# Hybrid attention and GLA encoder layer: softmax left unscaled, all linear q and k through the seven-product units, out projection split 6 and 10

## The chip, the cores and the metric

One core of one Trainium2 chip runs the whole layer. The metric is the device time of one execution in microseconds; the kernel before has a median of 2158.83 us over three runs.

## The reference

One encoder layer over 512 tokens of width 2048, in float32. A projection of 6176 columns feeds 16 softmax heads of 64 (group A) and four heads of gated linear attention, GLA (group B). Their outputs are concatenated, projected by `w_out`, added to the input, and followed by a SwiGLU of width 5632 and a last RMSNorm.

```
h = rmsnorm(x, attn_norm_w)
aq, ak, av, gq, gk, gv, gr, glr = split(h @ w_in)
# group A: three (window, dilation) patterns per head, merged by their softmax denominators
attn = sum_i softmax_i(lse)[i] * softmax(q k_i^T / 8 + bias) v_i
# group B: chunked gated linear attention, forward and backward, q and k of 4 heads x 128
o = gla(gq * 128**-0.5, gk, gv, gate_fwd) + flip(gla(flip(...), gate_bwd))
gla_out = rmsnorm_per_head(o) * gla_norm_w * silu(gr)
x = x + concat(attn, gla_out) @ w_out
x = x + (silu(h2 @ w_gate) * (h2 @ w_up)) @ w_down        # h2 = rmsnorm(x, ffn_norm_w)
return rmsnorm(x, final_norm_w)
```

Because all three patterns of a head are merged by their denominators, a head is one softmax over 512 keys with a bias that counts the patterns. The kernel computes it so.

## The kernel before

The schedule is written out by hand: the order in the program is the order on each engine. Every operand of a large product is split into a rounded high part (ScalarE, `act.copy`) and a low part (VectorE, a subtraction), and each product is three matmuls: high by high, high by low, low by high.

**Jobs.** A job (`run_job`) is a direct product over 16 blocks of 128 rows with four PSUM banks; one block of weights is a *half* of 12 matmuls with 512 columns. The stream `st` loads weights ahead on SP's queue and splits them. In the order of time: two jobs for the softmax heads' v; the Front stage (below); job "A", which computes the second 256 columns of the linear q and of the linear k directly and whose results `evac_gqk` scales and stores to `gqd`; two jobs for the linear v (`evac_gv`); the first half (rows 0 to 7 of `mixh`, the softmax heads' results) of the out projection for the column blocks 1, 2 and 3; the out projection of block 0 over all 16 rows; the second half of blocks 1, 2 and 3; then SwiGLU and the down projection.

**Front units.** `Front` computes 256 columns of `w_in` for all tokens as a *unit*: four pieces, in each of which two 2x2 block products are done with seven products instead of eight (`products`, lines 1548 and 1562: a matmul of 512 columns and one of 256 each). `evac7` combines the seven sums with ScalarE copies, VectorE additions and four accumulating DMAs of POOL's queue; `finish` multiplies by the row norms and stores to DRAM. Before there are 14 units: the gate r (4), the first half of linear q and k (2), the softmax q and k (8).

**Side work.** While a job runs, `run_side` advances a queue of generators by `rate` steps per half (`RATES`: 3.1 in job A and the gv jobs, 4.0 in the out jobs), after each of its four banks; every call first advances the generator at the head of `urgent` by one step. The side queue holds the low-rank gate (14 steps), then `attention`, then GLA (started in turns).

**Attention.** A step pair of `attention` is one *unit* `u` of 64 (16 heads x 4 query blocks). In unit u: scores on PE (`att_scores`, lines 630 and 631), bias and minimum on VectorE (`att_max`, L640), exponential with its row sum on ScalarE (`att_exp`, L648). Then the row is scaled by the reciprocal of its sum (`att_norm`: reciprocal, L651, and for even units the multiplication, L653, on VectorE; `att_scale` for odd units on ScalarE, L657). Then four transposes (`att_transpose`, L662), the rounded part (`att_round`, L670), the rest (`att_rest`, L676), the product with v for two units at a time (`att_av`, L686 and L687), a copy across partitions (`att_lift`, L696) and the sum into a head pair's result `mixf[pr]` (`att_mix`, L705), which is then split into `mixh[pr]`. `read_qk` loads the next pair's q and k by eight DMAs on POOL's queue (L569), `load_qk` splits them (L592, L588). GLA's last transposes stand at L1132, the split of its results at L922.

**Slots.** SBUF is cut into 36 slots of 512 columns (tiles `a`) and 33 of 1024 (tiles `b`), PSUM into 8 banks (`ps`); each is handed out in the order in which it came free, and its next writer waits for its last reader.

## Time and profile before

| | |
|---|---|
| median of three runs | 2158.83 us (2158.61 to 2159.88) |
| the profiled execution | 2159.02 us, span 2157.2 us |
| granted TensorE clock | 0.999 |
| HBM read and written | 287.47 MB and 66.39 MB |

The profile gives each engine's busy time (PE is TensorE's matmuls, PEld its weight loads, DVE VectorE, ACT ScalarE, POOL GpSimd, SP the queue that loads weights). Matmuls are pipelined and the profile models their ends, so the distance from one start to the next tells what a matmul costs, and the busy time does not. A wait row names the instruction that waited and the one that released it. A landing is the time from a DMA's issue to its completion.

### The profile page before, as it was taken

How to read it: one execution, taken by the hardware profiler on the slowest of the kernel's cores; microseconds unless marked ns; L12 is line 12 of the kernel's file. 1: busy time of each engine (PE TensorE's matmuls, PEld its weight loads, DVE VectorE, ACT ScalarE, POOL GpSimd, SP SyncE). 2: the span in 40 equal slices, each digit the busy share in tenths (PEclk: the TensorE clock that was granted, in tenths of full speed). 3: DMA queues.
4: the chain of work that ended last, by engine and by line, in shares of the span. 5: the costliest groups of instructions: out<-in, count | busy, mean ns of one | idle time of the engine just before them, and what ended most of it. 6: DMA issues, size and time to landing. Idle time of an engine off the chain costs nothing.

```text
span 2157.2 us, 35082 instructions
## 1 busy us (share of the span) xinstructions
PE 2145.5 (99%) x12714; PEld 1896.6 (88%) x12714; DVE 1843.6 (85%) x3187; ACT 1234.4 (57%) x2250; POOL 364.0 (17%) x501
## 2 busy tenths in 40 slices
PE   9999999999999999999999999999999999999998
PEld 7888888888888889888888888888888899999987
DVE  6699999688878788899999998999989888888885
ACT  8455555578876456455555555555555655555562
POOL 0011222211121110022112211221122220021300
PEclk9999999999999999999999999999999999999999
DMA  6367778846575863567677667776677885576982
GB/s 203 136 181 182 179 179 192 245 143 190 174 220 172 279 243 103 149 181 182 181 179 196 173 183 182 178 194 174 180 188 181 260 212 178 179 183 156 282 309 78
DMA packets 266203, 407.55 MB, mean 189 GB/s; under 512 B 19309, under 2 KB 163613, under 8 KB 266030
## 3 DMA queue, kind: packets, MB, share of 16 engines
q1 hardware_dynamic: 206238, 274.59, 39.8%
q0 software_dynamic: 59472, 130.19, 27.1%
q8 instruction: 100, 1.64, 0.3%
q14 instruction: 73, 0.60, 0.1%
q10 hardware_dynamic: 320, 0.53, 0.1%
HBM read 287.47 MB, written 66.39 MB: 164 GB/s over the span
## 4 chain that ended last, share of the span: by engine, by line
PE 56%; DMA 1%; issue 1%; DVE 1%; POOL 0%; ACT 0%; DVEq 0%; ACTq 0%; POOLq 0%
PE ps L1562 25%; PE ps L1548 12%; PE ps L1926 5%; PE ps L1927 5%; PE ps L1925 5%; PE ps L346 1%; PE ps L348 1%; PE ps L347 1%; PE ps L2122 1%; PE ps L2121 1%; PE ps L2120 1%; DMA gd<-b 1%; DMA b<-a 0%; POOL xd L1806 0%; DVE b L1471 0%
## 5 line engine op out<-in xcount | busy, mean ns | idle before, releaser
L1466 ACT CAST b<-b 128x1024 fp32r<-128x1024 f32 (+1 forms) x585 | 533.8, 944 | 386.4 <-DVE b L1471 193.1
L1471 DVE TENSOR_TENSOR b<-b,b 128x1024 fp32r<-128x1024 f32 (+1 forms) x585 | 614.0, 1084 | 34.4 <-ACT b L1466 22.9
L1562 PE MATMUL ps<-b,b 128*128 128x512 f32 x1708 | 500.7, 393 | 0.4 <-ACT b L1466 0.2
L1562 PE MATMUL ps<-a,b 128*128 128x512 f32 x1428 | 418.7, 393 | 0.3 <-DVE b L1582 0.2
L1562 PEld LDWEIGHTS ps<-b,b 128*128 128x128 f32 x1708 | 289.4, 188 | 32.6 <-ACT b L1466 0.6
L1548 PEld LDWEIGHTS ps<-b,b 128*128 128x128 f32 x1708 | 280.6, 190 | 40.8
L1548 PE MATMUL ps<-b,b 128*128 128x256 f32 x1708 | 307.4, 280 | 0.0
L1548 PEld LDWEIGHTS ps<-a,b 128*128 128x128 f32 x1428 | 236.9, 189 | 38.0 <-DVE b L1471 0.5
L1562 PEld LDWEIGHTS ps<-a,b 128*128 128x128 f32 x1428 | 238.5, 188 | 24.1 <-issue 0.6
L1548 PE MATMUL ps<-a,b 128*128 128x256 f32 x1428 | 256.6, 280 | 0.1
L1453 DVE TENSOR_TENSOR b<-b 128x512 f32<-128x512 f32 x268 | 183.6, 685 | 19.0 <-PE ps L1927 7.3
L1926 PE MATMUL ps<-b,b 128*128 128x256 f32 x624 | 176.6, 283 | 0.0
L1927 PE MATMUL ps<-b,b 128*128 128x256 f32 x624 | 176.6, 283 | 0.0
L1925 PE MATMUL ps<-b,b 128*128 128x256 f32 x624 | 176.6, 283 | 0.0
L346 PE MATMUL ps<-b,b 128*128 128x512 f32 x332 | 133.8, 403 | 0.1
L348 PE MATMUL ps<-b,b 128*128 128x512 f32 x332 | 129.8, 391 | 0.1
L347 PE MATMUL ps<-b,b 128*128 128x512 f32 x332 | 129.5, 390 | 0.0
L1454 DVE TENSOR_TENSOR b<-b,b 128x256 f32<-128x256 f32 x268 | 114.0, 425 | 9.3
L1455 DVE TENSOR_TENSOR b<-b,b 128x256 f32<-128x256 f32 x268 | 114.0, 425 | 9.2
L1927 PEld LDWEIGHTS ps<-b,b 128*128 128x128 f32 x624 | 119.8, 192 | 0.0
L1925 PEld LDWEIGHTS ps<-b,b 128*128 128x128 f32 x624 | 119.8, 192 | 0.0
L1926 PEld LDWEIGHTS ps<-b,b 128*128 128x128 f32 x624 | 119.8, 192 | 0.0
(308 smaller groups left out, 4039.8 us busy)
## 6 DMA issues: line engine op xcount, KB each, us to landing
b<-in_w_gate_dram SPq DMA_DIRECT2D x109, 512.0 KB, 3.7
b<-in_w_up_dram SPq DMA_DIRECT2D x88, 512.0 KB, 3.8
b<-in_w_down_dram SPq DMA_DIRECT2D x88, 512.0 KB, 5.4
b<-in_w_in_dram SPq DMA_DIRECT2D x86, 512.0 KB, 3.8
b<-a POOLq DMA_DIRECT2D x168, 256.0 KB, 4.5
b<-in_w_out_dram SPq DMA_DIRECT2D x32, 512.0 KB, 6.3
gd<-b POOLq DMA_DIRECT2D x22, 512.0 KB, 4.0
b<-gd SPq DMA_DIRECT2D x22, 512.0 KB, 8.3
```

What stands on the lines that cost most here:

```text
L346: mm(o, xh.t[:, c], wh.t[:, w], start=first and not on, stop=False, skip_group_check=on)
L347: mm(o, xh.t[:, c], wl.t[:, w], start=False, stop=False, skip_group_check=on)
L348: mm(o, xl.t[:, c], wh.t[:, w], start=False, stop=last, skip_group_check=on)
L1453: dve.tensor_tensor(s_[:, :, 0:2], r[:, :, 1:3], r[:, :, 0:1].to_broadcast(shape), op=OP.add)
L1454: dve.tensor_tensor(s_[:, :, 2], s_[:, :, 0], r[:, :, 2], op=OP.add)
L1466: act.copy(o, src)
L1471: dve.tensor_tensor(o, src, h, op=OP.subtract)
L1548: mm(o, wl, xh, start=False, stop=end, skip_group_check=True)
L1562: mm(o.rearrange("p (s t) -> p s t", s=2), wh, x_, start=first and p == 0, stop=False, skip_group_check=True)
L1925: mm(o, xh[:, t], wh, start=first and h == 0, stop=False, skip_group_check=True)
L1926: mm(o, xh[:, t], wl, start=False, stop=False, skip_group_check=True)
L1927: mm(o, xl[:, t], wh, start=False, stop=last, skip_group_check=True)
```

## The change

- `att_norm` and `att_scale` are gone. The exponentials go unscaled through transposes and the product with v. Row sums are collected in eight columns per head pair. In the next pair's units: one reciprocal of the eight columns (slot 0), a PE transpose of them into a spare part of a PSUM bank and a copy to SBUF (`sums_across`, slot 1), a DMA to DRAM (`sums_out`, slot 2), two DMAs that read them back, each broadcast to 64 partitions (`rows_in`, slots 2 and 3), one multiplication of the pair's result (`scaled`, slot 6), and the split (`split_mix`, slot 7).
- The transposes, the rest, the product with v, the lift and the mix move one unit forward; the loop has 69 instead of 71 units.
- The last pair's multiplication and split are a generator of their own on `urgent`, which first lets ten steps pass (`last_pair`).
- `read_qk` and `scan_operands` issue their DMAs one at a time, two in a unit, instead of all at once.
- Job A is gone; the second half of the linear q and k become two more Front units (16 in all). The first gv job takes over what was issued in job A (low-rank gate, start of attention, `load_qk(0)`, `load_v(0)`, the late Front unit), and the rate of the gv jobs is 4.5 instead of 3.1.
- The first out job (column block 1) takes rows 0 to 5 instead of 0 to 7, its second part rows 6 to 15.

```diff
         def att_exp(u):
             L = AT[u]
-            act.activation(L.t, L.t, AF.Exp, scale=-1.0, bias=am[u % 4], accum_out=asum[u % 4])
-
-        def att_norm(u):
-            dve.reciprocal(ar[u % 4], asum[u % 4])
-            if u % 2 == 0:
-                dve.tensor_scalar(AT[u].t, AT[u].t, ar[u % 4], None, op0=OP.mult)
-
-        def att_scale(u):
-            if u % 2:
-                act.activation(AT[u].t, AT[u].t, AF.Copy, scale=ar[u % 4])
+            act.activation(L.t, L.t, AF.Exp, scale=-1.0, bias=am[u % 4], accum_out=asum[u // 8 % 2][:, u % 8:u % 8 + 1])
+
+        def sums_across(b):
+            pe.transpose(b.t[0:8, 256:384], inv, idn)
+            dve.tensor_copy(line8, b.t[0:8, 256:384])
+
+        def sums_out(pr):
+            pool.dma_start(out=rd[pr], in_=line8)
+            rows[pr] = s2.get()
+
+        def rows_in(pr, n):
+            src = rd[pr, 4 * n:4 * n + 4].rearrange("j p -> (j p)")[None]
+            pool.dma_start(out=rows[pr].t[64 * n:64 * n + 64], in_=src.to_broadcast([64, 512]))
+
+        def scaled(pr):
+            v = lambda o: o.t.rearrange("p (b c) -> p b c", c=P)
+            f, r = mixf[pr], rows.pop(pr)
+            dve.tensor_tensor(v(f), v(f), v(r)[:, :, ::-1], op=OP.mult)
+            put(r)
+
+        def split_mix(pr):
+            f, (hi, lo) = mixf.pop(pr), s4.pair() if pr > 4 else hilo()
+            act.copy(hi.t, f.t)
+            yield
+            dve.tensor_tensor(lo.t, f.t, hi.f, op=OP.subtract)
+            put(f)
+            mixh[pr] = hi, lo
+
+        def last_pair(pr):
+            for n in range(LATE):      # LATE = 10
+                yield
+            scaled(pr)
+            yield
+            yield from split_mix(pr)
...
-            for u in range(UNITS + 7):
+            reads = iter(())
+            for u in range(UNITS + 5):
...
-                    if u % 8 == 1:
-                        read_qk(h // 2 + 1)
+                    if u % 8 == 0:
+                        for _ in reads:
+                            pass
+                        reads = read_qk(h // 2 + 1)
+                    next(reads, None)
...
-                run(att_scale, u - 3)
-                run(att_round, u - 4)
+                run(att_round, u - 3)
                 run(att_exp, u - 1)
+                if u % 2 == 0:
+                    run(att_lift, (u - 6) // 2, UNITS // 2)
+                pr, s_ = divmod(u, 8)
+                pr -= 1
+                if pr >= 0 and s_ == 2:
+                    sums_out(pr)
+                if pr >= 0 and s_ == 3:
+                    rows_in(pr, 1)
...
                 yield
-                run(att_norm, u - 2)
-                run(att_transpose, u - 3)
+                next(reads, None)
+                run(att_transpose, u - 2)
+                if u % 2:
+                    run(att_av, (u - 5) // 2, UNITS // 2)
+                run(att_rest, u - 3)
+                run(att_max, u)
                 if u % 2 == 0:
-                    run(att_av, (u - 6) // 2, UNITS // 2)
-                run(att_rest, u - 4)
-                run(att_max, u)
-                if u % 2:
-                    run(att_mix, (u - 7) // 2, UNITS // 2)
+                    run(att_mix, (u - 6) // 2, UNITS // 2)
+                if pr >= 0 and s_ == 0:
+                    dve.reciprocal(inv, asum[pr % 2])
+                if pr >= 0 and s_ == 1:
+                    sums_across(OT[(u - 5) // 2][0])
+                if pr >= 0 and s_ == 2:
+                    rows_in(pr, 0)
+                if pr >= 0 and s_ == 6:
+                    scaled(pr)
...
+            urgent.append(last_pair(NH // 2 - 1))
...
-        RATES = (3.1, 4.0)
+        RATES = (4.5, 4.0)
-        seg = [(w_in, C_GQ + 256), (w_in, C_GK + 256)]
-        job("A", [piece512(seg, None, k) for k in range(0, KT, 2)], list(range(KT)), acts_h,
-            evac_gqk, rate=RATES[0], start=gstart, before=before_first, limit=3)
         for pr in range(2):
             j = job("B", [piece512(w_in, C_GV + pr * 512, k) for k in range(0, KT, 2)], list(range(KT)), acts_h,
-                    evac_gv(pr), rate=RATES[0],
-                    before=(lambda i: load_gates() if i == 12 else None) if pr else None)
+                    evac_gv(pr), rate=RATES[0], start=None if pr else gstart, limit=3,
+                    before=(lambda i: load_gates() if i == 12 else None) if pr else before_first)
...
         for c in (1, 2, 3):
-            job_out(c, 0, 8, evac_out(c, True), rate=RATES[1], start=start_out(c))
+            job_out(c, 0, 6 if c == 1 else 8, evac_out(c, True), rate=RATES[1], start=start_out(c))
...
-            j = job_out(c, 8, KT, evac_out(c), rate=1.0, before=before_out(c))
+            j = job_out(c, 6 if c == 1 else 8, KT, evac_out(c), rate=1.0, before=before_out(c))
...
                 self.units = [(w_in, C_GR + g * 256) for g in range(4)] + [(w_in, C_GQ), (w_in, C_GK)] + \
+                    [(w_in, C_GQ + 256), (w_in, C_GK + 256)] + \
                     [(w_in, c + g * 256) for g in range(4) for c in (C_AQ, C_AK)]
```

More of the change, by code (lines that the diff above doesn't have):

```diff
@@ L618, in layer @@
         am = [small[:, 56 + i:57 + i] for i in range(4)]
-        asum = [small[:, 60 + i:61 + i] for i in range(4)]
-        ar = [small[:, 64 + i:65 + i] for i in range(4)]
+        asum = small[:, 60:68], small[:, 32:40]
+        inv = small[:, 40:48]
+        line8 = wrow1[0:8]
+        rd = dr.tile([NH // 2, 8, P], F32, name="rd")
+        rows = {}
         UNITS = 4 * NH
+        LATE = 10
         def att_scores(u):
@@ L758, in attention @@
+                if pr >= 0 and s_ == 1:
[4 more added lines that the diff above has]
+                    scaled(pr)
+                next(mixed, None)
+                if 31 <= u < 34:
+                    load_v(1, ((0,), (1,), (2, 3))[u - 31])
+                if u == 43:
+                    reads = scan_operands()
                 if u == 55:
@@ L844, in gate_weights @@
             G["gw"] = [G.pop(d) for d in range(2)]
[L846 to L847 removed]
+        gfd = dr.tile([4, P, 1024], F32, name="gfd")
         gvd = dr.tile([4, P, 1024], F32, name="gvd")
[L850 to L860 removed]
         def load_gla(h):
@@ L1403, in layer @@
             j.fine = True
-        j.drop = lambda k: drop_mix(k) if k < 8 else None
-        for j in jobs[n_front + 3:]:
+        j.drop = lambda k: drop_mix(k) if k < 6 else None
+        for j in jobs[n_front + 2:]:
             j.lead = lambda i: AHEAD + 4
-        jobs[n_front + 3].lead = lambda i: AHEAD + min(4, 3 + i)
+        jobs[n_front + 2].lead = lambda i: AHEAD + min(4, 3 + i)
         for c in (1, 2, 3):
-            j = job_out(c, 8, KT, evac_out(c), rate=1.0, before=before_out(c))
+            j = job_out(c, 6 if c == 1 else 8, KT, evac_out(c), rate=1.0, before=before_out(c))
+            if c == 1:
+                j.drop = lambda k: drop_mix(k) if k < 8 else None
         j.drop = drop_mix
@@ L1709, in do @@
                         dve.tensor_tensor(c_.t, c_.t, r, op=OP.mult)
-                    pool.dma_start(out=grd[u] if u < 4 else gfd[u - 4] if u < 6 else qkd[u - 6], in_=c)
+                    pool.dma_start(out=grd[u] if u < 4 else gfd[u - 4] if u < 8 else qkd[u - 8], in_=c)
                     put(c_)
@@ L1739, in run @@
                         if q == 1:
-                            read_qk(0)
+                            for _ in read_qk(0):
+                                pass
                         if q == 2:
```

47 lines of the change are left out of this document (12 added, 35 removed).

## The prediction

> **What bounds the kernel now.** I read the page's first lines, then the busy times by stage, then a stretch of the PE timeline, then who waits in the attention stage. The page:
>
> ```profile
> span 2157.2 us, 35082 instructions
> PE 2145.5 (99%) x12714; PEld 1896.6 (88%) x12714; DVE 1843.6 (85%) x3187; ACT 1234.4 (57%) x2250; POOL 364.0 (17%) x501
> ```
>
> The end is set by PE. PE ends are modelled, so the busy share alone proves little; I go by stages, whose edges are the first matmuls of the jobs (columns: stretch, length, busy time and count of each engine, clock, DMA share, GB/s):
>
> ```profile
> 60.70:104.20 43.50, 43.50 (x193) 36.03 (x192) 25.60 (x52) 17.15 (x34) 2.16 (x5) 1.00 0.43 145
> 104.20:123.70 19.50, 19.50 (x113) 17.09 (x113) 17.44 (x28) 10.09 (x17) 2.09 (x4) 1.00 0.66 216
> 182.20:201.70 19.50, 19.50 (x114) 17.12 (x113) 18.53 (x30) 10.41 (x18) 4.08 (x5) 1.00 0.73 182
> 104.20:377.90 273.70, 273.43 (x1569) 239.74 (x1569) 251.76 (x400) 144.32 (x238) 57.96 (x75) 1.00 0.74 184
> 377.90:448.90 71.00, 71.00 (x364) 57.95 (x364) 51.87 (x114) 46.62 (x99) 14.34 (x26) 1.00 0.69 200
> 448.90:526.40 77.50, 77.50 (x435) 66.21 (x434) 64.87 (x154) 60.60 (x129) 18.65 (x36) 1.00 0.62 184
> 603.40:628.00 24.60, 24.60 (x120) 20.61 (x119) 14.63 (x26) 19.28 (x34) 3.03 (x6) 1.00 0.79 257
> 699.70:760.50 60.80, 60.80 (x292) 51.27 (x291) 46.04 (x101) 27.93 (x72) 10.98 (x20) 1.00 0.85 283
> ```
>
> In order: the second linear v job (192 matmuls of 512 columns, no attention beside it), one Front unit, another, all 14 Front units, the direct q, k job, the first gv job, the first out job, the last full out job. The v job costs 43.5 / 192 = 0.2266 us a matmul; each Front unit 19.5, on average 273.7 / 14 = 19.55. DVE has 17.4 in one unit and 18.5 in the other, and both last 19.50: PE's stream sets the pace, not DVE. In the first gv job, 24 softmax units go beside 192 matmuls. Does anything hold PE there?
>
> ```profile
> POOL a L569 <- DVE a L705: 44.6, 3, 19.2
> ACT b L670 <- PE ps L662: 14.5, 19, 1.7
> DVE a L640 <- PE ps L631: 6.0, 9, 1.5
> DVE b L676 <- ACT b L670: 3.0, 5, 1.0
> PE ps L662 <- DVE b L880: 0.2, 1, 0.2
> ```
>
> (The last row is from PE's own waits over the three jobs, 377.9 to 603.4.) PE waited 0.2 us in all; ACT and DVE wait for PE. So the time follows the matmul work, as long as DVE and ACT keep up. What an attention unit costs PE:
>
> ```profile
> 487.44 0.39 PE L630 MATMUL ps<-a,a 128*128 128x512 f32 x1
> 487.89 0.39 PE L346 MATMUL ps<-a,b 128*128 128x512 f32 x1
> ...
> 488.58 0.60 PE L662 MATMUL ps<-idn,a 128*128 128x128 f32 x4
> 488.93 0.48 PE L346 MATMUL ps<-a,b 128*128 128x512 f32 x1
> ...
> 491.92 0.36 PE L686 MATMUL ps<-b,b 128*128 128x256 f32 x1
> 492.95 0.40 PE L346 MATMUL ps<-a,b 128*128 128x512 f32 x1
> ```
>
> Start to start: scores 0.45, four transposes 0.35, the product with v 1.03 for two units: 0.45 + 0.35 + 0.52 = 1.32 us a unit.
>
> **Linear q, k as units: the main term.** The direct job's 192 matmuls go. Undisturbed they cost 43.5. In place: its 71.0 us less 17 scores (7.7), 14 groups of transposes (4.9), 6 products with v (6.2) and 32 low-rank matmuls of 0.2266 (7.3) leaves 45.0. I take 44.5. Two Front units come: 2 x 19.55 = 39.1. They are like the 14 that stand there (four pieces, 56 matmuls of 512 and 56 of 256 columns each); their DVE, ACT and POOL work lies in the units' own time as in the others. Net **-5.4** (bounds -4.4 and -5.9).
>
> By the Trainium skill (Perfetto Trace Analysis, section Identifying the Most-Contended Engine) matmul busy time is a poor measure, LDWEIGHTS busy time is the better one, and other engines go by occupancy. By that, the Front stage has PE at 239.74 / 273.7 = 88% and DVE at 92%, and DVE would be what a new unit pays for: 251.76 / 14 = 18.0 us each, 36.0 for both, a sum lower by 3.1 us. The two unit rows, equal in length with DVE 1.1 us apart, speak against it here.
>
> **Softmax unscaled: off PE's path.** DVE and ACT in the first gv job:
>
> ```profile
> L676 DVE TENSOR_TENSOR b<-ps,b 128x512 fp32r<-128x512 f32 x24 | 16.4, 684 | 3.2 <-ACT b L670 3.0
> L218 DVE TENSOR_TENSOR a<-b,a 128x512 fp32r<-128x512 f32 x13 | 8.9, 683 | 0.1
> L653 DVE TENSOR_SCALAR a<-a,small 128x512 f32<-128x512 f32 x12 | 5.9, 488 | 0.4
> L705 DVE TENSOR_TENSOR a<-ps,a 64x256 f32<-64x256 f32 x12 | 5.0, 420 | 0.2
> L651 DVE RECIPROCAL small<-small 128x1 f32<-128x1 f32 x24 | 3.8, 157 | 0.1
> L657 ACT ACTIVATE a<-a,small 128x512 f32<-128x512 f32 x12 | 8.6, 716 | 1.9 <-DVE small L651 1.9
> ```
>
> Gone per unit: (5.9 + 3.8) / 24 = 0.40 us of DVE and 8.6 / 24 = 0.36 of ACT. Added per pair of heads (8 units): one multiplication (0.684), one reciprocal (0.157), one copy of the row block (at most 0.42), so 0.16 a unit. All of it is hidden behind PE, so worth 0 by itself. It pays for the next edit.
>
> **Rate 4.5 instead of 3.1.** Attention now has 32 halves, not 48. A half is 12 matmuls, 44.5 / 16 = 2.8 us; 36 units go into 16 halves, so a unit comes every (44.5 + 36 x 1.32) / 36 = 2.56 us instead of 77.5 / 24 = 3.2. DVE in the gv row without the 16 low parts of the stream (16 x 0.683 = 10.9) is (64.87 - 10.9) / 24 = 2.25 a unit; less 0.40, plus 0.16 makes 2.01. For 36 units and the stream: 72.4 + 10.9 = 83.3 of 92.0, 91%, against 84% before. The Front stage runs at 92% with PE at pace, but there DVE works further ahead. Here the loop transposes - round (L670) - rest (L676) - free bank - scores has one and a half units of slack, 4.8 us before and 3.8 after, for about 1.5 us of work; a burst on DVE will now and then be late. I put +1.0 (0 to 3).
>
> **Rows.** Eight new PE transposes, 0.35 / 4 = 0.09 each: +0.7 (0 to 1.2, as each also waits for the reciprocal half a unit ahead of it). New waits: POOL's row reads wait for their write to land, and behind them in POOL's queue stand the last two reads of the next pair's q, k; DVE's multiplication waits for the rows, and behind it stand every rest and maximum, for which PE waits. Landings nearest to them:
>
> ```profile
> L569 POOL DMA_DIRECT2D a<-qkd x64: 516/523/1239, 373.3 to 548.3; - x64
> DMA to landing us min/median/max: 2.5/5.5/10.2
> ...
> L799 POOL DMA_DIRECT2D a<-in_gla_gate_w_fwd_dram x1: 503/503/503, 538.4 to 538.4; - x1
> DMA to landing us min/median/max: 1.9/2.0/2.1
> ```
>
> Write: 0.52 + 2.0; three more issues in the queue, 1.6; a 64-row read of 128 KB, as L569's: 5.5. Sum 9.6 us. From the write's place (slot 2 of the next pair) to the multiplication (second half of slot 6) are 4.5 units, 11.5 us. Hidden, with 1.9 to spare: 0. The Trainium skill (DMA: Bandwidth & Descriptors, section Anatomy of one DMA) fits such a DMA by 2.0 us plus bytes over 436e3 per us: 2.3 for 128 KB, an estimate under which the sum is 0 as well and the spare 5.1; this trace's median of 5.5 for that size decides, and leaves a rival.
>
> **Moved to the first gv job's start.** Low-rank steps, loads of v, the first pair and the late unit keep their halves, with fewer microseconds between:
>
> ```profile
> 375.20 2.34 SPq L600 DMA_DIRECT2D b<-vd  x4
> b<-vd SPq DMA_DIRECT2D x4, 512.0 KB, 12.8
> 395.84 3.28 POOL L569 DMA_DIRECT2D a<-qkd  x5
> ```
>
> SP runs ahead: v is requested 2.7 us before the job and there about 13 us later; its first product comes at step 26 of 4.5 a half, half 5.8, over 16 us in. Hidden. The second pair's reads leave POOL 18 us into the job, behind the last unit's accumulating DMAs; the attention now starts at half 3.1 (14 low-rank steps), about 16 us in, and needs them four units later, at about 25, when the first have just landed (18 + 5.5, at worst 28). Up to 2 us of ACT waiting; PE has a unit or so in hand: within the +1.0.
>
> **Out jobs.** 6 and 10 instead of 8 and 8 leaves the matmuls as they are: 0. But the steps: before, 48 x 3.1 less the three unfilled job ends (0.8 each) gives 146.5 for 14 + 142; after, 32 x 4.5 less 2.25 gives 141.75 for 14 + 138. The tail in the first out job is 9.5 and 10.25 steps, and that job yields 23 steps, not 31. GLA is 8.75 steps, 2.2 halves, about 6.0 us later against the last full out job, which reads its last results in the last two halves (2 x 12 x 0.2266 = 5.4 before 760.5, at 755.1):
>
> ```profile
> 744.03 1.04 PE L1132 MATMUL ps<-idn,b 128*128 128x128 f32 x8
> 747.39 1.29 DVE L922 TENSOR_TENSOR b<-a,b 128x512 fp32r<-128x512 f32 x2
> ```
>
> Ready at 748.7, read from 755.1: 6.4 of slack, 0.4 left: +0.3 (0 to 1.5). The last pair's finish takes 13 urgent steps, three halves, and ends about with the first out job; its first reader is the second out job's seventh half, 16 us on: 0.
>
> **Sum:** -5.4 + 1.0 + 0.7 + 0.3 = **-3.4**. The profiled execution took 2159.02 (span 2157.2 and 1.8 around it), 0.2 over the median of 2158.83: 2155.6 by the one, 2155.4 by the other. I say **2155.4**. What this kernel's measurement can tell from no change is about 0.2%, 4.3 us: below 2154.5 is faster, above 2163.1 slower.
>
> **Rivals.**
> - *DVE becomes the bound of attention (slower).* If the handoffs leave DVE idle for as long per unit as before, (77.5 - 64.87) / 24 = 0.53 us, 36 units need 83.3 + 19.1 = 102.4 instead of 92.0: 0.29 a unit, 64 units, +18.5: 2174. If only the named waits stay (6.0 + 3.0 in 24 units, 0.38): 97.0, +8.9: 2164. It decides from a unit pitch of 2.56 + 7.7 / 64 = 2.68 us. For: 91%. Against: those waits are for PE itself and shrink when PE is faster. Chance 0.11.
> - *Rows late.* With the worst landing (10.2) the chain is 14.3, 2.8 us late; DVE's free 9% of 11.5 covers 1.0. In four of eight pairs: +7.2, 2162.6. For: the reads of the first pairs took 8 to 10. Against: the median. Chance 0.08.
> - *GLA's end waits for DVE* at the last out halves: up to 3 us more, 2158. Chance 0.08.
> - *More comes off:* new units at DVE's 18.0 us, the rule weighed above, or no new wait at all: 2152.3 to 2153.9. Chance 0.13.
> - That the edit fails to do what it says can hardly be: the scaling is linear and moves as a whole.
>
> **Numbers.** Forecast 0.60, own range 2153.6 to 2157.5 (a third of it under 2154.5, through the bounds of the main term: 0.22). Faster 0.22 + 0.13 = 0.35; slower: 0.09 of the first rival, 0.03 of the second, 0.01 of the third = 0.13; within 0.2% the rest, 0.52. The range 2152.6 to 2161.0 leaves out most of the DVE rival and half of the late rows (0.14) and little below.
>
> **What would show it.** Right: 16 Front units of 19.5 us; two gv jobs of about 92 us each; PE waits there under 3 us; no L653, L657; the row multiplication without idle time before it. Wrong: PE idle ahead of scores or transposes with DVE as releaser, DVE over 94% there, idle time of microseconds before the multiplication, a PE gap at the end of the last full out job.

## The result, and the profile after

The changed kernel takes **2163.18 us** (median of 20 executions, 2159.93 to 2165.8) against 2158.95 (2158.09 to 2160.99) for the kernel before in the same measurement: ratio 1.0017, 95% interval 1.0010 to 1.0024. That is 0.17% slower, a small change but clear of the noise. Forecast was 2155.4, range 2152.6 to 2161.0. The profiled execution took 2164.56; a second profiled execution (e15, below) 2162.84. The page's first lines after:

```profile
span 2162.7 us, 35260 instructions
PE 2144.2 (99%) x12754; PEld 1895.8 (88%) x12754; DVE 1852.5 (86%) x3153; ACT 1226.1 (57%) x2236; POOL 382.8 (18%) x531
```

PE's busy time fell by 1.3 us and the span rose by 5.5: PE stands idle where it did not before. Busy times by stage (stretch, length, then each engine, clock, DMA share, GB/s): the 16 Front units, the two gv jobs, the first, second and third out job, the last full out job:

```profile
104.30:420.00 315.70, 313.28 (x1793) 274.32 (x1792) 288.04 (x458) 164.72 (x272) 65.31 (x84) 1.00 0.73 180
420.00:510.50 90.50, 88.14 (x485) 72.54 (x484) 67.61 (x142) 62.34 (x137) 26.67 (x50) 1.00 0.69 202
510.50:604.10 93.60, 92.85 (x546) 79.69 (x545) 82.46 (x178) 75.64 (x168) 24.98 (x48) 1.00 0.69 213
604.20:626.20 22.00, 21.45 (x113) 17.96 (x112) 11.55 (x22) 17.28 (x31) 3.81 (x7) 1.00 0.83 275
626.20:659.90 33.70, 32.12 (x155) 26.94 (x154) 32.10 (x61) 20.17 (x41) 9.77 (x15) 1.00 0.69 204
659.90:693.30 33.40, 33.33 (x164) 27.81 (x163) 25.73 (x56) 22.18 (x58) 7.86 (x15) 1.00 0.52 166
693.30:761.10 67.80, 67.14 (x332) 55.99 (x331) 52.23 (x111) 35.21 (x85) 10.32 (x19) 1.00 0.80 267
```

PE's busy time is 2.4 us short of the length in the first gv job, 0.8 in the second, and 0.5 and 1.6 in the first two out jobs. DVE is busy 75% and 88% of the gv jobs: not full.

Since PE's ends are modelled, I measure its delays by starts. The **stall** of a stage is the sum, over its PE instructions, of the distance from one start to the next less the usual (median) distance for that pair of instructions. Negative sums are the noise of this. The usual distance blends matmuls with and without a group of transposes ahead of them, and the matmul behind such a group needs 0.31 us to the next start instead of 0.23; so the absolute sums are too high, in both kernels alike, and only the differences count. In us:

| stage | before | after | e15 (after again) | e3 softmax only | e10 sums moved | e16 sums, finish moved |
|---|---|---|---|---|---|---|
| Front | -0.3 | 2.6 | -0.5 | 0.8 | -1.8 | -0.7 |
| direct q, k job | 1.5 | - | - | 1.6 | - | - |
| gv jobs | 2.5 + 3.1 | 5.8 + 4.7 | 5.9 + 4.8 | 2.8 + 3.0 | 5.5 + 4.6 | 4.1 + 4.7 |
| first out job | 0.2 | 1.2 | 1.3 | 0.5 | 1.2 | 1.2 |
| second, third, last full out job | 5.0 | 7.5 | 7.5 | 6.7 | 5.3 | 5.4 |

So attention has 3.3 to 3.5 us more of stalls than before (10.5 and 10.7 against 7.2) and the out jobs 3.5 more (8.7 and 8.8 against 5.2); both repeat. Front's 2.6 does not. If the usual distance is taken for three instructions in a row, which keeps apart what follows transposes, attention goes from 1.4 to 4.6 (4.8 in e15) and the out jobs from 1.8 to 5.1: the same differences within 0.2. The named waits of PE in the first gv job (two rows), the second (one) and from the second to the last full out job (one), and last the only one of these out jobs before the change:

```profile
PE ps L635 <- DVE b L705: 2.0, 2, 1.1
PE ps L867 <- DVE a L861: 0.4, 1, 0.4
...
PE ps L635 <- DVE b L705: 0.8, 1, 0.8
...
PE ps L1066 <- DVE a L1072: 2.0, 2, 1.6
...
PE ps L1037 <- DVE a L1043: 0.7, 1, 0.7
```

L635 is the scores, L705 the rest, whose late end keeps a PSUM bank; L867 is the low-rank gate's start, L1066 (before: L1037) are GLA's transposes. The largest stalls: 640.7 us (1.75, GLA), 458.6 (1.28), 449.8 (1.04), 586.0 (1.00), 604.7 (0.71, at the change of jobs, where attention's transposes wait for a bank of the gv results), 700.1 (0.53, GLA), 421.8 (0.52, low-rank gate). What lies behind the one at 449.8? Waits of all engines from 415 to 460:

```profile
POOL b L1637 <- DMA b<-a: 16.1, 2, 10.7
ACT a L593 <- DMA a<-qkd: 13.2, 5, 4.9
DVE a L589 <- ACT a L593: 8.6, 3, 4.0
```

and the same place in POOL's timeline:

```profile
427.59 0.88 POOL L1636 DMA_DIRECT2D b<-a  x1
439.19 0.86 POOL L1637 DMA_DIRECT2D b<-a  x1 [10.72 <-DMA b<-a]
439.74 1.21 POOL L1638 DMA_DIRECT2D b<-a  x1
440.29 1.22 POOL L1739 DMA_DIRECT2D qkd<-b  x1
440.84 3.28 POOL L569 DMA_DIRECT2D a<-qkd  x5
```

The last Front unit's third accumulating DMA waits 10.7 us for the second to land. Behind it, in order, stand a unit's store and the second head pair's reads; ScalarE waits for these reads, DVE for ScalarE, and the rest stands behind that on DVE. The kernel before has the same wait on POOL (11.0 us) in its direct job, where it stalled nothing. At 586 it is a burst on DVE: split, stream, key splits, all ahead of one rest.

```profile
583.04 0.68 DVE L705 TENSOR_TENSOR b<-ps,b 128x512 fp32r<-128x512 f32 x1
583.64 0.68 DVE L645 CUSTOM_DVE_ANT_0 a<-ps,b 128x512 f32<-128x512 f32 x1
...
584.25 0.68 DVE L677 TENSOR_TENSOR b<-a,b 128x512 fp32r<-128x512 f32 x1
584.96 1.41 DVE L589 SCALAR_TENSOR_TENSOR a<-a,a 64x512 fp32r<-64x512 f32 x2
586.29 0.68 DVE L705 TENSOR_TENSOR b<-ps,b 128x512 fp32r<-128x512 f32 x1
```

At 640.7 DVE has SwiGLU's first sums (L1550) and the stream (L218) ahead of GLA's step L1072, for which PE waits until 642.67:

```profile
640.50 0.88 DVE L1550 TENSOR_TENSOR b<-b 128x256 f32<-128x256 f32 x2
641.29 0.68 DVE L218 TENSOR_TENSOR b<-b,b 128x512 fp32r<-128x512 f32 x1
641.89 0.72 DVE L1072 COPY_PREDICATED a<-masks,ps 128x512 f32<-128x512 uint32 x1
```

### The profile page after: what moved, and what is told of

Same layout as the page of the kernel before. It is cut to its first block, busy times and chain, and to the rows that moved or that the text cites. A ratio compares the mean times of both kernels' runs of the same rounds, so it can differ in the third digit from the quotient of the medians.

```text
span 2162.7 us, 35260 instructions
## 1 busy us (share of the span) xinstructions
PE 2144.2 (99%) x12754; PEld 1895.8 (88%) x12754; DVE 1852.5 (86%) x3153; ACT 1226.1 (57%) x2236; POOL 382.8 (18%) x531
## 4 chain that ended last, share of the span: by engine, by line
PE 58%; DVE 0%; DMA 0%; issue 0%; ACT 0%; DVEq 0%; ACTq 0%
PE ps L1590 24%; PE ps L1576 12%; PE ps L1957 5%; PE ps L1956 5%; PE ps L1955 5%; PE ps L348 1%; PE ps L346 1%; PE ps L347 1%; PE ps L2151 1%; PE ps L2150 1%; PE ps L2152 1%; DMA gd<-b 0%; DVE b L1499 0%; DVE a L2183 0%; DVE a L1610 0%
## 5 line engine op out<-in xcount | busy, mean ns | idle before, releaser
L1494 ACT CAST b<-b 128x1024 fp32r<-128x1024 f32 (+1 forms) x601 | 549.1, 945 | 403.0 <-DVE b L1499 204.0
L1499 DVE TENSOR_TENSOR b<-b,b 128x1024 fp32r<-128x1024 f32 (+1 forms) x601 | 630.7, 1084 | 30.8 <-ACT b L1494 18.9
L1590 PE MATMUL ps<-b,b 128*128 128x512 f32 x1760 | 517.3, 393 | 0.4 <-ACT b L1494 0.2
L1590 PE MATMUL ps<-a,b 128*128 128x512 f32 x1488 | 436.7, 394 | 2.4 <-DVE b L1610 2.4
L1590 PEld LDWEIGHTS ps<-b,b 128*128 128x128 f32 x1760 | 298.2, 188 | 33.2 <-ACT b L1494 0.7
L1576 PEld LDWEIGHTS ps<-b,b 128*128 128x128 f32 x1760 | 289.9, 190 | 42.3
L1576 PE MATMUL ps<-b,b 128*128 128x256 f32 x1760 | 318.0, 280 | 0.0
L1576 PEld LDWEIGHTS ps<-a,b 128*128 128x128 f32 x1488 | 246.6, 189 | 39.4 <-DVE b L1499 0.7
L1590 PEld LDWEIGHTS ps<-a,b 128*128 128x128 f32 x1488 | 248.8, 188 | 28.1 <-ACT b L1494 2.3
L1576 PE MATMUL ps<-a,b 128*128 128x256 f32 x1488 | 267.6, 280 | 0.2 <-DVE b L1499 0.2
L1955 PE MATMUL ps<-b,b 128*128 128x256 f32 x624 | 176.6, 283 | 0.0
L1956 PE MATMUL ps<-b,b 128*128 128x256 f32 x624 | 176.6, 283 | 0.0
L1957 PE MATMUL ps<-b,b 128*128 128x256 f32 x624 | 176.6, 283 | 0.0
L346 PE MATMUL ps<-b,b 128*128 128x512 f32 x340 | 137.7, 405 | 0.0
L348 PE MATMUL ps<-b,b 128*128 128x512 f32 x340 | 133.0, 391 | 0.1
L347 PE MATMUL ps<-b,b 128*128 128x512 f32 x340 | 132.6, 390 | 0.0
L1483 DVE TENSOR_TENSOR b<-b,b 128x256 f32<-128x256 f32 x276 | 117.4, 425 | 9.5
L1482 DVE TENSOR_TENSOR b<-b,b 128x256 f32<-128x256 f32 x276 | 117.3, 425 | 9.6
L1635 POOL DMA_DIRECT2D b<-a x58 | 50.3, 867 | 412.7 <-ACT b L1494 256.7
L1955 PEld LDWEIGHTS ps<-b,b 128*128 128x128 f32 x624 | 119.8, 192 | 0.0
L1956 PEld LDWEIGHTS ps<-b,b 128*128 128x128 f32 x624 | 119.8, 192 | 0.0
```

Source lines behind the costliest of these rows:

```text
L346: mm(o, xh.t[:, c], wh.t[:, w], start=first and not on, stop=False, skip_group_check=on)
L347: mm(o, xh.t[:, c], wl.t[:, w], start=False, stop=False, skip_group_check=on)
L348: mm(o, xl.t[:, c], wh.t[:, w], start=False, stop=last, skip_group_check=on)
L1483: dve.tensor_tensor(s_[:, :, 3], s_[:, :, 2], r[:, :, 3], op=OP.add)
L1494: act.copy(o, src)
L1499: dve.tensor_tensor(o, src, h, op=OP.subtract)
```

## The experiments

Each kernel was timed beside the kernel before on the same chip, whose median was 2158.6 to 2159.3.

**e1, two more units and nothing else** (kernel before; the direct job stays):

```diff
...
+                    [(w_in, C_GQ + 256), (w_in, C_GK + 256)] + \
...
```

> The kernel before, with the two Front units of the second half of the linear q and k added, and the direct job kept (both compute the same values, those of the units are not read). If a unit costs its matmuls alone, 2 x 19.55 = 39.1 us come on top: about 2198. If the units wait for the landings of the accumulating DMAs, as the trace after shows (PE waits 2.4 us there, 16 units took 315.7 us instead of 312.8), it is 40.5 to 42.5: 2199.5 to 2201.5.

2198.42 us (ratio 1.0180, 1.0166 to 1.0194): +39.2. Front after its 16 units:

```profile
104.30:418.20 313.90, 313.17 (x1793) 274.31 (x1792) 288.33 (x459) 164.86 (x271) 65.06 (x84) 1.00 0.74 181
```

A new unit costs its matmuls, 19.6 us; the term of 39.1 was right, and DVE's 18.0 is not the price.

**e2, the change with the softmax scaled as before** (kernel before with 16 units, no direct job and the split 6 and 10; rate 4.64, so that attention ends at the same place; of the edit only the rate is shown):

```diff
...
-        RATES = (3.1, 4.0)
+        RATES = (4.64, 4.0)
...
```

> The kernel before with the jobs of the change (no direct job, 16 units, out split 6 and 10), but with the softmax rows scaled as before; rate 4.64, as its attention has four steps more. If the unscaled softmax is what makes the dense attention possible, DVE now needs (2.25 x 37.1 + 10.9) / 37.1 = 2.54 us a unit where PE needs 2.52, and this is slower than the change by 5 us or more, 2168 or above. If the rows' path through DRAM costs more than the scaling did, it is faster than the change: 2158 to 2162.

2163.87 us (1.0022, 1.0014 to 1.0031), in neither branch. The second gv job:

```profile
508.10:605.70 97.60, 95.86 (x551) 79.53 (x551) 91.43 (x221) 88.15 (x191) 17.63 (x34) 1.00 0.63 191
```

DVE 94%, ACT 90%, and 97.6 us instead of 93.6: its stalls are 7.7 instead of 4.7. But the first out job is left with 98 instead of 111 PE instructions, and the out jobs stall 7.0 instead of 8.7. In sum (3.3 less 1.7) the unscaled softmax is worth some 1.6 us of stalls at this density, not the jump the theory asked for.

**e3, the softmax part alone on the kernel before** (rows, `last_pair`, rate 3.1, direct job kept; the second half of v is requested two units later than in the change).

> The kernel before with the softmax part of the change alone (rows on the pair's result, one unit less of depth, reads issued one at a time, the last pair's finish spread; direct job, 14 units, rate 3.1 and split 8 and 8 kept; the second half of v requested two units later than in the change). If the rows are hidden, only the eight transposes show: 2159 to 2160. If POOL's queue, held by the rows, delays the reads of q and k and with them PE: 2162 or more.

2162.64 us (1.0016, 1.0007 to 1.0025): +3.4, not near zero. But the reads of q and k are not why, as direct job and gv jobs hardly change (stalls +0.2; DVE 59.9 instead of 64.9 in the first, close to the forecast 0.24 a unit). The out jobs lose 2.0, at GLA's transposes and products:

```profile
PE ps L1079 <- DVE a L1085: 0.8, 1, 0.8
PE ps L1104 <- DVE a L998: 0.7, 1, 0.7
```

Here GLA is not late: its first transposes start 26.4 us after the first out job, against 30.1 before and 33.5 after the change. So a later GLA is not needed for a loss in the out jobs. And the two parts do not add: e2, the jobs without the softmax part, costs 4.6, e3 3.4, both together 4.2.

**e4, first out job with 8 rows again:**

```diff
-            job_out(c, 0, 6 if c == 1 else 8, evac_out(c, True), rate=RATES[1], start=start_out(c))
+            job_out(c, 0, 8, evac_out(c, True), rate=RATES[1], start=start_out(c))
...
```

> The change with the first out job over eight rows as before. GLA gets eight steps back, so if it is GLA's lateness that costs in the out jobs, this is faster than the change by 1 to 3 us: about 2161. If the last pair's rows are what is late (they landed at 624.6 in the trace after, at the end of that job), the job's last half now waits for them, split included: slower by 2 to 5 us, 2165 to 2168.

2166.2 us (1.0032, 1.0020 to 1.0045). The first out job's stalls are 7.5: its last half waits for the last pair's two parts,

```profile
PEld ps L346 <- ACT b L675: 2.4, 1, 2.4
PEld ps L348 <- DVE b L677: 2.1, 1, 2.1
```

while the three jobs behind it stall 4.7 instead of 7.5. The split 6 and 10 saves 6 us in the first out job (part of them lost here because the clock is at half for 6.8 us, see the last section), and behind it 2.8 more are lost than with 8 and 8.

**e5, is DVE too full?** In the gv jobs the stream's subtraction is left out, and the high part of the weights stands in its place in the second matmul:

```diff
-                    dve.tensor_tensor(h[3].t, raw.t[:, h[1] * 512:(h[1] + 1) * 512], h[2].f, op=OP.subtract)
+                    if not jobs[n_front].first <= n < jobs[n_front + 2].first:
+                        dve.tensor_tensor(h[3].t, raw.t[:, h[1] * 512:(h[1] + 1) * 512], h[2].f, op=OP.subtract)
...
```

> The changed kernel, but in the two gv jobs the low part of each block of weights is not computed: the high part stands in its place in the second matmul, so PE has the same matmuls and DVE 32 subtractions of 0.683 us (21.9 us) less in the two jobs. Theory 'DVE is too full': the stalls of the changed kernel's gv jobs (matmul starts later than the usual distance: 5.8 and 4.7 us) come from bursts on DVE ahead of the rest; with 21.9 of its 150.1 us gone they fall to 2 us a job or less, the two jobs last 184.1 - 6 = 178 us, the kernel 2157 to 2159. Rival 'single waits': the stalls come from transfers that land late and from the order of single steps (the second head pair's reads, the late unit's finish); they stay at 9 or more of 10.5, the kernel at 2162 to 2164.

2162.32 us (1.0015, 1.0007 to 1.0024). By stages, and PE's one named wait in the first of them (L637 and L707 are the scores and the rest here):

```profile
417.70:509.50 91.80, 89.56 (x485) 73.85 (x484) 59.01 (x127) 61.95 (x137) 26.77 (x50) 0.98 0.69 196
509.50:602.20 92.70, 92.70 (x546) 79.74 (x545) 74.21 (x163) 75.04 (x168) 24.80 (x48) 1.00 0.70 215
...
PE ps L637 <- DVE b L707: 2.2, 1, 2.2
```

With 16.9 us less on DVE the second job loses its burst at 586 (stalls 4.7 to 3.6), but the first gets worse (7.0): DVE, idle for a third of it, is still late at 449, where ScalarE waits for the reads. Part of the 7.0 is the clock, at half for 3.4 us after that wait (0.98 in the row; see the last section). "Too full" falls for the first job; the single waits stay, but for the one at 586.

**e6, the second pair's reads asked for earlier, on POOL's queue, and the late unit's finish at half 11:**

```diff
...
                         if q == 2:
+                            for _ in read_qk(1):
+                                pass
                             gla_operands()
...
-            if i == 7:
+            if i == 11:
                 fr.late()
...
```

> The changed kernel with two single waits taken away: the second head pair's q, k are requested in the last Front unit's third piece, ahead of that unit's accumulating DMAs in POOL's queue, and the late unit's finish moves from half 7 to half 11 of the first gv job. Theory 'single waits': the stalls of 1.04 us at 449.8 and 1.28 us at 458.6 go, the first gv job's stalls fall from 5.8 to about 3.3, the kernel takes 2160.5 to 2161.5. Rival 'DVE is too full': the same delay appears at the next burst, the job still lasts 90 to 90.5 and the kernel 2162.5 to 2164.

2170.16 us (1.0052, 1.0039 to 1.0064), worse than either theory. Waits from 430 to 455:

```profile
DVE b L705 <- DMA qkd<-b: 11.8, 1, 11.8
...
POOL b L1637 <- DMA b<-a: 10.5, 1, 10.5
```

The reads went ahead, the accumulating DMAs and the store went back by 6.7 us, and the rest's output slot was still held by that store: one stall of 8.4 us.

**e7, fewer of SwiGLU's first sums in the second out job** (1.25 a half to 0.25, in the third 1.5 to 2.5).

> The changed kernel with fewer of SwiGLU's first sums on DVE in the second out job (0.25 a half instead of 1.25; 2.5 instead of 1.5 a half in the third). Theory 'the last pair's finish and these sums meet GLA's first chain on DVE': the stall of 1.75 us at 640.7 falls to 0.9 or less as before the change, the second out job lasts 32.5 to 33.0 instead of 33.8, the kernel 2162 to 2162.5 with the third job unchanged. Rival: the third job's chain is met instead, what is saved in the second is lost there: 2163 to 2164.

2163.6 us (1.0020, 1.0011 to 1.0028). The second job's stalls fell as expected, 2.6 to 1.1; the last full one's rose from 3.5 to 5.4. The sums matter, and moving them to the wrong place gives it back (in the last full out job, not in the third, where the rival had it).

**e8, 4.6 steps a half in the out jobs.**

> The changed kernel with 4.6 instead of 4.0 steps a half in the out jobs, so that GLA, which starts about two halves later than before the change, catches up before the last full out job. Theory 'GLA late': the stalls of the last full out job (3.5 us, 1.5 before the change) fall to 2 or less, the kernel takes 2160.5 to 2162. Rival 'too dense': GLA's chains wait for DVE more often in the jobs before; stalls of the three first out jobs rise from 5.2 to 7 or more, the kernel takes 2163.5 to 2167.

2168.21 us (1.0039, 1.0026 to 1.0053). The last full job fell to 2.1, the second rose from 2.6 to 8.6: the rival.

**e9, the second pair's reads on SP's queue, and the finish at half 11:**

```diff
-                            pool.dma_start(out=qkr[pr][i][n].f[r], in_=src)
+                            (sp if pr == 1 else pool).dma_start(out=qkr[pr][i][n].f[r], in_=src)
...
```

> The changed kernel, in which the second head pair's eight reads of q, k go through SP's queue instead of POOL's (so that they no longer stand behind the last Front unit's accumulating DMAs), and the late unit's finish moves from half 7 to half 11 of the first gv job. Theory 'single waits': the stalls at 446 to 450 us (0.3 to 2.4 in the runs so far) and at 458 us (1.0 to 1.5) both go; the first gv job's stalls fall from 5.8 to 3.0 to 3.6 and its length from 90.5 to 88 or a little less; the kernel 2.5 us below the changed one, 2160 to 2161, with less spread between executions. Rival 'PE's own handoffs': with a unit every 2.5 us scores wait there whatever lands; the job's stalls stay at 5 or more and the kernel at 2162.5 to 2164.

2162.26 us (1.0019, 1.0010 to 1.0029). The stall at 458 is gone; at 446.5 there are 2.6 us, with a new releaser, the slot of the store that still stands on POOL's queue:

```profile
ACT b L699 <- DMA qkd<-b: 4.8, 1, 4.8
```

**e10, the sums moved off GLA's chains:**

```diff
-            a = ... {0: 0.5, 1: 1.25, 2: 1.5}[n - n_in + 3] ...
-            j.ahead = (lambda i: 1.5 if i < 6 else 2.75) if n == n_in else lambda i, a=a: a
+            a = ... {0: 0.75, 1: 0.5, 2: 1.0}[n - n_in + 3] ...
+            j.ahead = (lambda i: 0.5 if i < 3 else 3.4) if n == n_in else lambda i, a=a: a
```

> The changed kernel with SwiGLU's first sums on DVE moved off GLA's chains: 0.75, 0.5 and 1.0 a half in the first three out jobs instead of 0.5, 1.25 and 1.5, in the last full out job 0.5 in its first three halves and 3.4 after them instead of 1.5 and 2.75. Theory 'these sums meet GLA's chains, which start two halves later than before the change': the stall at 640.7 (1.75 us) falls to 0.9 or less, those at 667.8 (0.34), 694.4 (0.52) and 700.1 (0.53) go; stalls of the three jobs from the second out job on fall from 7.5 to 5 (before the change: 5.0), the kernel 2160.5 to 2162. Rival 'paid later': the denser sums in the last full out job hold up GLA's last chains, its stalls rise above 4, the kernel 2163 to 2165.

2159.95 us (1.0005, 0.9996 to 1.0013): 3.2 below the changed kernel. The three jobs and their one named PE wait:

```profile
622.30:654.90 32.60, 32.15 (x155) 26.96 (x154) 29.91 (x55) 20.09 (x41) 9.20 (x14) 1.00 0.62 179
654.90:687.90 33.00, 33.00 (x164) 27.83 (x163) 24.87 (x55) 22.27 (x59) 7.36 (x14) 1.00 0.57 174
687.90:755.10 67.20, 66.69 (x331) 56.02 (x330) 54.04 (x118) 34.68 (x84) 10.72 (x19) 1.00 0.83 271
...
PE ps L1066 <- DVE a L1072: 0.8, 2, 0.5
```

Stalls 5.3 instead of 7.5, the 640.7 stall 0.6. The stages explain 2.2 of the 3.2 us.

**e11, e9 and e10 together.**

> The two changes of the runs e9 and e10 together. If the waits they take away are separate places of PE's stream, the gains add: gv stalls of 7.5 to 8 instead of 10.5, out stalls of 6.2 instead of 8.7, together 5 us below the changed kernel: 2157.5 to 2159.5, no slower than the kernel before. If stalls only move from one burst to the next, it takes 2161 or more.

2162.41 us (1.0016, 1.0007 to 1.0025). The out jobs kept e10's gain (5.4); the stall at 447 was 3.3, and the first gv job's sum 9.6 (the last section says why it is so much more). In its three executions with a mean clock of 0.999 it took 2158.1 to 2160.1, the forecast of added gains within 0.6; in the eight with 0.997 or 0.998, 2162.1 to 2166.9.

**e12, that store on SP's queue too:**

```diff
...
-                    pool.dma_start(out=grd[u] if u < 4 else gfd[u - 4] if u < 8 else qkd[u - 8], in_=c)
+                    (sp if u == 14 else pool).dma_start(out=grd[u] if u < 4 else gfd[u - 4] if u < 8 else qkd[u - 8], in_=c)
...
```

> As e9 (the second pair's reads on SP's queue, the late unit's finish at half 11), and the store of the last but one Front unit goes through SP's queue too. Theory 'POOL's queue': in e9 the stall at 446.5 us (2.6) stayed because ScalarE's rounding waited 4.8 us for a slot that this store still held, and the store stood behind the last unit's third accumulating DMA, which waits 10.6 us. With both off that queue the stall at 446 goes (under 0.5), the first gv job's stalls fall from 6.0 to 3.0 to 3.6, its length to 87.5 to 88.5, the kernel 2159.5 to 2160.5. Rival 'PE's own handoffs or another transfer': a stall of over 1 us stays within 5 us of that place with another releaser; the kernel 2162 or more.

2164.32 us (1.0023, 1.0014 to 1.0032). The slot is not waited for any more, the reads for 0.4 us; 1.7 us of stall at 446.5 remain, now behind a load of the bias, which stands on SP's queue behind what was moved there:

```profile
DVE a L645 <- DMA b<-line: 3.9, 1, 3.9
```

**e13, e12 and e10 together.**

> The edits of e12 and of e10 (SwiGLU's first sums moved off GLA's chains). If both causes are right and separate: stalls of the gv jobs 7.5 to 8.3 and of the jobs from the second out job to the last full one 5.3 as in e10, the kernel 2156.5 to 2158, faster than the kernel before by 1 to 2.5 us. If the first gv job keeps its stall: 2159.5 to 2162.

2162.84 us (1.0015, 1.0006 to 1.0023): the first gv job keeps its stall (2.4 at 449).

**e14, the kernel before with e10's rates.**

> The kernel before with e10's rates of SwiGLU's first sums (nothing else). Theory 'the sums met GLA because the change moved GLA by two halves': here the three jobs lose little, their stalls stay at 4.5 to 5.0, the kernel 2158.5 to 2159.3. Rival 'the sums cost GLA in any kernel': it gains as much as e10 did, 2155.5 to 2157, and the change is no part of that cost.

2158.71 us (0.9998, 0.9989 to 1.0007), stalls of the three jobs 4.75 instead of 5.0. The meeting of these sums with GLA belongs to the change.

**e15, the changed kernel again.**

> The changed kernel as it is, timed beside the others. Theory 'single waits': the same stalls at the same places (640.7, 586.0, 604.7 within 0.05 us of the first profile, counted from the start of their jobs), while the one at 446 to 450 and those of the Front stage differ; 2162 to 2164.

2162.84 us (1.0018, 1.0009 to 1.0027). The stalls at GLA, 586 and 604.7 repeat to 0.02 us, those at 448 (1.18) and in Front (-0.5 instead of 2.6) differ.

**e16, e10 and the finish at half 11.**

> The changed kernel with two edits that each removed the stall they aimed at: the late unit's finish at half 11 (the one at 455 to 458 us, 1.0 to 1.5) and e10's rates of SwiGLU's sums. Theory 'single waits add': the first gv job's stalls fall from e10's 5.4 to about 4.4, the out jobs stay as in e10, the kernel 2158.8 to 2160. Rival: with the finish gone the wait at 446 to 450 us grows by as much, as it seemed to in e9; the kernel 2160 to 2162.

**2158.84 us** (1.0001, 0.9992 to 1.0010), the best version with the change, and no different from the kernel before. The first gv job takes 88.8 us with stalls of 4.1. In this execution the stall at 446 to 450 was under 0.25; why it was small there is not shown.

**e17 and e18, as e16 with the attention five and eight steps later, rate 4.75:**

```diff
             side.append(slow(low_rank()))
+            side.append(iter(range(5)))
...
-        RATES = (4.5, 4.0)
+        RATES = (4.75, 4.0)
...
```

> As e16, and the attention starts five steps later (about one half, 2.8 us) in the first gv job, with a rate of 4.75 instead of 4.5 so that it ends no later. Theory 'the first head pairs meet the Front stage's last transfers': these 2.8 us cover most of the wait at 446 to 450 us, the first gv job's stalls fall below 3.5, the kernel 2157 to 2159. Rival 'density': at 4.75 steps a half the bursts on DVE cost more, the second gv job's stalls rise from 4.7 to 6 or more and the kernel takes 2160 to 2164.

> As e17 with eight steps instead of five (1.7 halves, 4.7 us later). Theory as there: the wait at 446 to 450 us is gone (under 0.3), 2157 to 2158.5; if GLA's later start costs what it did in the change, 0.5 to 2 us more than e17. Rival 'density': as e17, 2160 to 2164.

2166.1 us (1.0032, 1.0021 to 1.0044) and 2166.12 (1.0033, 1.0021 to 1.0044). At 446 to 450 nothing of 0.25 us is left in either; but e16, from which they start, had nothing there in its profile either, so that the start against Front's last transfers was the cause there is likely and not shown. The first gv job stalls 4.9 and 5.9 us, not under 3.5: at 477 to 480 us the late unit's finish (1.2 us on DVE) now meets the first pair's split and key splits, and 1.6 us are lost there in both. The rival holds for the total: the second gv job's stalls rise to 10.7 and 11.2. But their reason is again no full DVE (84% of that job in e17). It is, in e17's second gv job, a slot held by a store of the first job's results:

```profile
PE ps L635 <- DVE b L705: 5.2, 4, 1.8
...
DVE b L705 <- DMA gvd<-b: 4.3, 1, 4.3
```

## Why the prediction was wrong

Against e15, whose Front stage was undisturbed (span 2161.0, +3.8 on the profile of before), the sum reads as follows (stalls by three instructions in a row, so that the price of transposes is not among them):

| term | predicted | measured |
|---|---|---|
| direct job's matmuls out, two units in | -5.4 | -4.0 |
| dense attention's handoffs | +1.0 (0 to 3) | +3.4 |
| eight row transposes | +0.7 | +0.9 |
| GLA and the last pair in the out jobs | +0.3 (0 to 1.5) | +3.3 |
| the rest (start, later stages) | 0 | +0.2 |
| sum | -3.4 | +3.8 |

- **Main term: right in kind, 1.4 too large, just outside its bounds (-4.4 and -5.9).** Front grew by 313.2 - 273.7 = 39.5. Of the two values for the direct job's matmuls, 43.5 and 45.0, the first was right. The second took a group of transposes at 0.35 us, up to the next start; but the matmul behind it needs 0.31 to the start after, instead of 0.23 (in the kernel before from 488.93, a row of the prediction, to the row below). With 0.43 a group, 14 groups hold 1.1 of the 1.5 us between the two values; they are attention's, and moved on with it.

```profile
489.24 0.40 PE L347 MATMUL ps<-a,b 128*128 128x512 f32 x1
```

- **The step that failed first: "I put +1.0 (0 to 3)" for handoffs.** The argument was a share, 91% of DVE, and a slack per unit. The share came out lower (150.1 of 184.1 us, 82%, and 88% in the second job), yet the stalls rose by 3.4, because they are not spread over the units: four single places carry them (421.8, 449.8, 458.6 and 586.0 us, 3.8 together; none of over 0.35 us lay there before). The paragraph on the first gv job's start had found one, late reads with up to 2 us of ACT waiting, and let PE's lead hide it. It put their landing at 18 + 5.5 = 23.5 us into the job, with the median of all 64 reads; these very reads had taken 8.3 to 8.9 us in the kernel before. In the changed kernel they leave POOL at 20.8 and take 6.7 us and more, and ScalarE, idle from 25.9, has the first at 28.8: 3.0 us of waiting, of which 1.04 reach PE. The place cost 0.3 to 2.4 us in the profiles of kernels that left this place alone (under 0.25 in e16).
- **The step that failed second: "+0.3" for GLA.** I priced only GLA's end, and there it was right: the last split ends at 754.43 + 1.29 = 755.7, just when it is read, and no gap follows. What was not priced is everything else on DVE along GLA's way. Of the 3.3, 2.5 lie in the second to the last full out job: there GLA's chains, two halves nearer to the last full out job's end, meet SwiGLU's sums; moving the sums brings 2.1 of them back (e10), and next to nothing in the kernel before (e14). That the lateness makes them meet is not shown: e3 loses 2.0 with GLA 4 us earlier. The other 0.8 is in the first out job, most of it attention's wait at 604.7, which belongs to the first step. The last split:

```profile
754.43 1.29 DVE L951 TENSOR_TENSOR b<-a,b 128x512 fp32r<-128x512 f32 x2
```

- **"Last pair's finish: 0"** was half right: with the split 6 and 10 it delays no reader (e4 shows 6 us without it), but its two DVE steps (L670 at 629.7 and L677 at 632.7, 1.35 us) stand ahead of the chain that is late at 640.7; what they cost alone was not tested.
- **Rows: right.** The multiplication has no idle time before it, and a row transpose costs 0.03 us to the next start and 0.08 more behind it, 0.11 in all, near the 0.09 of the forecast:

```profile
L670 DVE TENSOR_TENSOR a<-a,a 128x512 f32<-128x512 f32 x7 | 4.7, 674 | 0.0
L656 PE MATMUL ps<-idn,small 128*8 128x128 f32 x7 | 1.9, 272 | 0.0
```

- **Rivals.** DVE as the bound did not come (75% and 88%), and the gv jobs lasted 184.1 / 72 = 2.56 us a unit as forecast, below its threshold of 2.68; they took 90.5 and 93.6 where 92 each was forecast. That agreement is partly luck: the 184.1 hold the stalls, and the plain matmuls took less than assumed. Rows late did not come. "Slower" had 0.13 in all; the sign was lost to an addition of small waits that no single rival held. Named PE waits in the gv jobs were 3.2 us, against "under 3" and 0.2 before, with DVE as releaser: the sign of being wrong that the prediction named.
- Open: e16 still stalls 1.6 us more in the gv jobs and 1.4 more in the out jobs than before, which with the row transposes uses up the main term. The burst at 586 went only where work was left out (e5) or the attention came later (e17, e18), at a higher price elsewhere.

## What to carry to other kernels

When a job is taken away, its cover goes too: list what was issued beside it (transfers, stores whose slots are next in line, another engine's bursts) and ask for each what it meets after the move; DVE's busy shares of 75 and 88% said nothing on this. Look at every queue in order: here one transfer that waited 11 us on POOL's queue held a store, the store held a slot, and each repair uncovered or made another late transfer (the store in e6 and e9, the bias in e12). Move steps that are due late (sums, finishes) out of the way of a chain first; here two such moves together brought the kernel back to the time before, some 4 us (e16); up to 1 us of that is the wait at 446 to 450, which neither aimed at.

## What was not expected of the hardware

A pause of PE can cost more than its length. In e11 PE stood for 3.2 us, and the clock granted after it was 0.50 for 6 us; in e13 a pause of 2.2 us had the same sequel for over 3 us; in e9 a longer one, 2.5 us, had none (columns as above, the last but two is the clock):

```profile
447.50:450.70 3.20, 0.03 (x2) 0.03 (x1) 0.77 (x2) 1.39 (x4) 0.00 (x0) 0.89 0.77 266
450.70:452.70 2.00, 2.00 (x5) 1.61 (x6) 2.00 (x5) 1.98 (x6) 0.00 (x0) 0.50 0.02 6
...
454.70:456.70 2.00, 2.00 (x6) 1.61 (x5) 1.19 (x2) 1.24 (x4) 0.00 (x0) 0.50 0.00 0
...
449.40:451.70 2.30, 0.11 (x2) 0.04 (x1) 0.76 (x3) 0.00 (x1) 0.00 (x0) 0.97 1.05 290
451.70:454.00 2.30, 2.30 (x10) 2.20 (x11) 2.27 (x5) 2.05 (x5) 0.00 (x0) 0.50 0.43 160
...
446.00:449.50 3.50, 1.02 (x8) 0.82 (x8) 0.95 (x2) 1.57 (x4) 0.00 (x0) 1.00 0.77 251
449.50:452.00 2.50, 2.50 (x14) 2.05 (x14) 2.50 (x8) 2.48 (x7) 0.00 (x0) 1.00 0.18 39
```

What decides is where the pause lies. Inside the kernel every stretch at 0.50 lasted 3.4 us (e5, e8, e13), 6.8 (e4, e11, e18) or 10.2 (e6), and within one trace such stretches begin whole multiples of 3.413 us apart (in e11, the one at 450.02 begins 500 of them before the one at the kernel's end, at 2156.69). So I count fixed windows of 3.413 us back from that last one and add up PE's idle time in each. All seven windows at full clock with 2.0 us or more of idle time were followed by half clock, and none with 1.74 or less. The 2.2 us of e13 lie in one window almost whole (2.08); the 2.5 us of e9 straddle a boundary (1.3 and 1.2). Full clock came back after windows with at most 0.11 us of idle time (seven), not after those with 0.65 or more (five).

So the first gv job of e11, with its pause of 3.2 us, stalls 9.6 us in all, that of e16, without it, 4.1. It shows in the times as well: of e9's eleven executions the six with a mean clock of 0.999 have a median of 2161.2 us, the five with 0.997 or 0.998 one of 2166.0. A stall of two microseconds at a place that varies thus spreads the times of these variants (2158 to 2168) far more than those of the kernel before. The Trainium skill (TensorE: Matmul & The Clock Gate, Part 1) describes such a gate: half clock after an idle window of about 3.4 us, a window that runs freely, full clock after a busy one. The two levels, the length and the free phase agree with these traces; that 2.0 us of idle time in a window are enough does not follow from it, and here the traces decide.
